# A hybrid diffusion kernel on one core: row broadcasts as two rounded products, adaLN's PSUM bank lent out, heads' transposes in one run, fold's first run and transposes later

## The chip, the cores and the metric

The kernel runs on 1 core of one Trainium2 chip. The metric is the device time of one launch in microseconds (us), the median over runs. All arithmetic is to float32 accuracy. The engines have the profile's names: PE is TensorE (matmuls, with its weight loads as PEld), DVE is VectorE, ACT is ScalarE, POOL is GpSimd, SP is SyncE (which issues most of the transfers).

## The reference, cut to what matters

Two layers over 256 latent tokens and 256 context tokens of width 1024. The first has a convolution mixer, the second a bidirectional mLSTM with four heads of width 512. Each is followed by an MLP of inner width 4096, and each sub-layer is modulated by shifts, scales and gates that adaLN derives from a condition vector. Only the latent tokens are returned.

```python
def adaln(cvec, w, b):
    return jnp.split(jax.nn.silu(cvec) @ w + b, 6, axis=-1)       # sh1, sc1, g1, sh2, sc2, g2

def mlstm_features(u, ...):
    up = u @ w_up
    xm, z = up[..., :MLSTM_INNER], up[..., MLSTM_INNER:]
    xc = jax.nn.silu(dwconv(xm, w_conv) + b_conv)
    q, k, v = xc @ w_q, xc @ w_k, xm @ w_v
    gates = jnp.concatenate([q, k, v], axis=-1) @ w_gate + b_gate
    o = jax.nn.sigmoid(xm @ w_o + b_o)                             # the output gate

def mlstm_output(feats, h_f, h_b, gn_g, skip, w_down):
    hsum = of[..., :MLSTM_INNER] * from_heads(h_f) + of[..., MLSTM_INNER:] * from_heads(h_b)
    hn = normalise(hsum, per head) * gn_g
    return ((hn + skip * xc) * jax.nn.silu(z)) @ w_down

# each layer
h = layer_norm(ALPHA * h + g1 * y, ln1_g[i], ln1_b[i])
h = layer_norm(ALPHA * h + g2 * (jnp.square(jax.nn.relu(modulate(h, sh2, sc2) @ w1)) @ w2), ln2_g[i], ln2_b[i])
```

## The kernel before

**Products.** TensorE multiplies float32 operands either in full precision (tiles of type F32) or rounded (F32R). To keep accuracy in the rounded form, `split` makes of a float32 tile `x` a high part (a cast to F32R on ScalarE, L154) and a low part (`x` less the high part, on VectorE, L155). `mm3t` (L223 to L225) and its sisters (L185, L188, L189; L201, L212) then add up high × high, low × high and high × low in PSUM. Weights come from DRAM into a `raw` tile and are split into `wh` and `wl`, 1024 columns at a time, in four buffers each. A few small products are in full precision: the sums of adaLN, the row broadcasts below, the fold (below), and transposes, which are products with `ident`.

**Order.** Each engine runs its instructions in the order of the built program. The framework's scheduler builds that order from the order in which the code is written, from the buffers (an instruction that writes a tile waits for the last reader of the buffer), and from `tc.issue_after(a)`, which keeps an instruction behind `a`. DMAs on SP are issued in order as well. Generators (`yield`) weave stages into each other step by step: the table `Z.att` names which parts of the output gate (`o0` to `o3`, one for a head), of the scan (`G`, `W`, `A`), and of the down projection (`D0` to `D3`) run together.

**PSUM.** `psum(tag)` hands out banks of 128 × 512 floats: three `mm`, two `ln`, two `cv`, and one, `fl`, which the sums of adaLN and the fold use. A group of products into a bank waits until the last reader of that bank's former content is done.

**Stages,** by the profile's time: adaLN of layer 0 and the convolution's first projection to 150 us, its second projection and the first MLP to 570, the up projections to 690, the v projection (`wv`) to 900, queries, keys and scores head by head to 1182, the output gate together with attention and the down projection to 1453, norm and adaLN's last units to 1459, the last MLP to the end. The change touches these:

- *Fold.* The gates' pre-activations need `w_q` times its part of `w_gate`. Instead of a product with the activations, the kernel multiplies `w_q` transposed (`wqT`) by that part (`wgq`), 16 columns wide and so in four column groups at a time. The `wv` stage has 32 steps of 24 matmuls. `wgq_load` issues one group's loads at steps 1, 5, 12 and 19; `wgq_group(0)` (L876) runs the first group at step 3, and the later ones run further on. `wgq_last`, at step 27, copies the sum out of `fl` on ScalarE (L884) and transposes the copy by four products on PE (L887).
- *Row broadcasts.* `AdaV` gathers adaLN's gate of the second mixer on VectorE in tiles `acc` (S in the profile). `row` (L479) multiplies a full matrix of ones with each, in full precision, which sums over partitions and spreads the sum over all of them; VectorE adds that to the gate's row. It is issued where the output gate begins. `gate2` (L2013) does the same for the last MLP's gate, from the tile `F` and with a column of `fold` as weights, in the second quarter of the last MLP (c = 1).
- *Output gate.* `gate_o(h)` makes for each of two halves (d) a pair of groups (t = 0, 1) of 48 matmuls into two `mm` banks. VectorE reads each bank once, adding a bias (L1752), and ScalarE applies the sigmoid. The three `mm` banks thus serve pairs in turn.
- *Heads.* `attend(h)` normalises the head's output in two blocks (t = 0, 1), scaled on ScalarE (L1806), and transposes them by eight products (L1814) into two `ln` banks, t = 0 first. `down(h)` multiplies the result by `wdown`.
- *Last MLP.* Four quarters (c). `gemm(w1_1, ...)` (L201, L212) produces four blocks each into `mm` banks, which VectorE empties with an addition in `joined` (L218); then `w2_mm` adds into four banks of `ln` and `cv`. The helper `gemm` takes a table `spare` that names another bank for a block.

Of the kernel before, what the change touches and what calls it, by code (L numbers as in the profile page):

```python
# [14 lines left out]
P = 128  # L15
# [56 lines left out]
def hybrid_kernel(ctx: ExitStack, tc: tile.TileContext, xT, vecs_d, taps_d, bdw_d, ada0_w, ada_w, wg_d, pw1a, pw1, pw2, w1_0, w2_0,  # L72
# [61 lines left out]
    nc.gpsimd.iota(fe[:, 0:HL + 1], [[1, HL + 1]], base=0, **exact)  # L134
    ident = con.tile([P, P], F32, name="ident")
    make_identity(nc, ident)
    ones = con.tile([P, P], F32, name="ones")
    nc.vector.memset(ones, 1.0)
    inv_h = con.tile([P, P], F32, name="inv_h")
    nc.vector.memset(inv_h, 1.0 / DH)  # L140
# [80 lines left out]
    def mm3t(ps, xh, xl, wh, wl, start, stop):  # L221

        nc.tensor.matmul(ps, xh, wh, start=start, stop=False)  # L223
        nc.tensor.matmul(ps, xl, wh, start=False, stop=False)  # L224
        nc.tensor.matmul(ps, xh, wl, start=False, stop=stop)  # L225

    def kcol(w, kt):
        if isinstance(w[0], list):
# [183 lines left out]
    class AdaV:  # L412
# [62 lines left out]

        def row(self, i, dst):

            ps = psum()
            nc.tensor.matmul(ps, ones, self.acc[i], start=True, stop=True)  # L479
            nc.vector.tensor_tensor(dst, ps, dst, op=ALU.add)  # L480

    def ad(l, s, which):
        i = ["sh1", "sc1", "g1", "sh2", "sc2", "g2"].index(which)
# [395 lines left out]

    wqs_ps = []  # L880

    def wgq_last():
        qsb = tmp("F")
        nc.scalar.copy(qsb, wqs_ps[0])  # L884
        qtr = psum("fl")
        for b in range(4):
            nc.tensor.transpose(qtr[:, b * P:(b + 1) * P], qsb[:, b * P:(b + 1) * P], ident)  # L887
        nc.vector.tensor_copy(wgp[1].rearrange("p (j b) c -> p j b c", j=4)[:, :, :, 0:16],
                              qtr.rearrange("p (b j c) -> p j b c", b=4, j=4)[:, :, :, 0:16])
# [556 lines left out]
    vstep = 0  # L1446
    for _ in gemm_steps(wv, range(8), xm, T, v_epi):
        vstep += 1
        if vstep in (1, 5, 12, 19):
            wgq_load()  # L1450
        if vstep == 3:
            wgq_group(0)
        if vstep == 27:
            wgq_last()
        if vstep > ET:
            ada_n2.step()
        if vstep in (20, 28):
            xc_load(0 if vstep == 20 else 4)
# [95 lines left out]
    def decay(_):  # L1554
        gT = tmp("L")
        nc.scalar.copy(gT, gps)
        yield
        gk = psum("ln")
        for b in range(4):
            nc.tensor.matmul(gk[:, b * 16:(b + 1) * 16], gT[:, b * P:(b + 1) * P], foldg, start=True, stop=True)  # L1560
        gs = tmp("S")[:, 0:64].rearrange("p (b c) -> p b c", b=4)
        nc.vector.tensor_tensor(gs, gk[:, 0:64].rearrange("p (b c) -> p b c", b=4),
                                VA("b_gate").rearrange("p (b c) -> p b c", b=4), op=ALU.add)
        gb_ = [tmp("L"), tmp("E"), tmp("E")]
        g8 = [gb_[i // 3][:, (i % 3) * 4 * NG:(i % 3 + 1) * 4 * NG].rearrange("p (b c) -> p b c", b=4) for i in range(8)]
        ig, fg, bsb, ex, up1, cor, lf, fa = g8
        nc.vector.memset(ig, 0.0)
        nc.vector.memset(fg, 0.0)
        for d in range(2):
            nc.vector.tensor_copy(ig[:, :, 32 * d:32 * d + 4], gs[:, :, 8 * d:8 * d + 4])  # L1570
            nc.vector.tensor_copy(fg[:, :, 32 * d:32 * d + 4], gs[:, :, 8 * d + 4:8 * d + 8])


        nc.vector.scalar_tensor_tensor(fa, fg, -1.0, fg, op0=ALU.mult, op1=ALU.max)
        nc.scalar.activation(ex, fa, AF.Exp, scale=-1.0)
        nc.vector.tensor_scalar(up1, ex, 1.0, None, op0=ALU.add)
        nc.vector.scalar_tensor_tensor(cor, up1, -1.0, ex, op0=ALU.add, op1=ALU.subtract)
        nc.scalar.activation(lf, up1, AF.Ln)
        nc.vector.reciprocal(up1, up1)
        nc.vector.tensor_tensor(cor, cor, up1, op=ALU.mult)  # L1580
        nc.vector.tensor_tensor(lf, cor, lf, op=ALU.subtract)
        nc.vector.tensor_scalar(fa, fg, 0.0, None, op0=ALU.min)
        nc.vector.tensor_tensor(lf, lf, fa, op=ALU.add)

        nc.vector.memset(up1, 0.0)
        for d, (b0, b1, b2, b3) in ((0, (0, 1, 2, 3)), (1, (1, 0, 3, 2))):
            c = slice(32 * d, 32 if d == 0 else NG)
            nc.vector.tensor_copy(up1[:, b1, c], lf[:, b0, c])
            nc.vector.tensor_tensor(up1[:, b2, c], up1[:, b1, c], lf[:, b1, c], op=ALU.add)
            nc.vector.tensor_tensor(up1[:, b3, c], up1[:, b2, c], lf[:, b2, c], op=ALU.add)  # L1590
        yield
        yield
        yield
        yield
        bps = psum("ln")
        for d, cum in ((0, upper), (1, lower)):
            c = slice(32 * d, 32 if d == 0 else NG)
            reg = bps[:, 0:4 * NG].rearrange("p (b c) -> p b c", b=4)[:, :, c]
            nc.tensor.matmul(reg, cum, lf[:, :, c], start=True, stop=False)
            nc.tensor.matmul(reg, ones, up1[:, :, c], start=False, stop=True)  # L1600
        nc.vector.tensor_copy(bsb, bps[:, 0:4 * NG].rearrange("p (b c) -> p b c", b=4))
        nc.vector.tensor_tensor(acol, ig, bsb, op=ALU.subtract)

        yield
        aT = psum("ln")
        for b in range(4):
            nc.tensor.transpose(aT[:NG, b * P:(b + 1) * P], acol[:, b, :], ident)
        aR, mR = tmp("S"), tmp("S")
        nc.vector.tensor_copy(aR[:32, :], aT[:32, :])
        nc.vector.tensor_copy(aR[32:NG, LO], aT[32:NG, LO])  # L1610
        nc.vector.tensor_copy(aR[32:NG, HI], aT[32:NG, T - 1:C - 1:-1])
        nc.vector.tensor_tensor_scan(mR[:NG, :], aR[:NG, :], aR[:NG, :], 0.0, op0=ALU.max, op1=ALU.max)
        nc.vector.tensor_scalar(negm[:32, :], mR[:32, HI], -1.0, None, op0=ALU.mult)
        nc.vector.tensor_scalar(negm[32:NG, :], mR[32:NG, T - 1:C - 1:-1], -1.0, None, op0=ALU.mult)
        nc.scalar.dma_start(ng_dr, negm)
        bsbs.append(bsb)
        yield
# [112 lines left out]
    def gate_o(h):  # L1730

        for d in range(2):
            bo = rows(BO().rearrange("p a b -> p (a b)"), bo_d[h:h + 1, d * DH:(d + 1) * DH])
            pss = [psum() for _ in range(2)]
            if (h, d) == (1, 1):
                with tc.issue_after(loaded[0]):
                    nc.sync.dma_start(R, r_dr)
            for q in range(4):
                ws = preo if (h, d, q) == (0, 0, 0) else None
                if ws is None:  # L1740
                    raw = raw_load(wo[h, d, q])
                for i in range(2):
                    w = ws[i] if ws else split_w(raw[:, i * 1024:(i + 1) * 1024])
                    for t in range(2):
                        for k in range(2):
                            kt = 4 * q + 2 * i + k
                            sl = slice(k * 512, (k + 1) * 512)
                            mm3t(pss[t], xls[kt][0][:, BLK[t]], xls[kt][1][:, BLK[t]], w[0][:, sl], w[1][:, sl],
                                 kt == 0, kt == ET - 1)
                        if q == 3 and i == 1:  # L1750
                            og[h, d, t] = o_ = OG()
                            nc.vector.tensor_tensor(o_, pss[t], bo, op=ALU.add)  # L1752
                            nc.scalar.activation(o_, o_, AF.Sigmoid)
                    yield
# [12 lines left out]
    def attend(h):  # L1767
# [37 lines left out]
        for t in range(2):  # L1805
            nc.scalar.activation(hs[t], hs[t], AF.Identity, scale=mv[:, t, 2:3], bias=mv[:, t, 3:4])  # L1806
        yield
        yy[h] = []
        for jp in range(2):
            tr = psum("ln")  # L1810
            for jj in range(2):
                j = 2 * jp + jj
                for t in range(2):
                    nc.tensor.transpose(tr[:, jj * C + t * P:jj * C + (t + 1) * P], hs[t][:, j * P:(j + 1) * P], ident)  # L1814
            y = og[h, 1, jp]
            for jj in range(2):
                j, sl = 2 * jp + jj, slice(jj * C, (jj + 1) * C)
# [10 lines left out]
    def down(h):  # L1828
# [13 lines left out]

        def mms(ps, ws, hf, t, first, last):
            for kt in range(4):
                mm3t(ps, yy[h][kt][0][:, BLK[t]], yy[h][kt][1][:, BLK[t]], *ws[hf][kt], first and kt == 0, last and kt == 3)

        if h == 0:
            for hf, ws in enumerate(load()):
# [86 lines left out]
            pre1[m] = split_w(rx[:, (m % 2) * 1024:(m % 2 + 1) * 1024])  # L1935
    ca, cb = comb(1, "ln1_g1", "ln1_b1", "sc2", "sh2", (1,))
    ada_n3 = Ada(1, 10, 2)
    u2 = [X(F32R) for _ in range(DT)]

    def turn(t, g_, tag="ln"):  # L1940
# [69 lines left out]
    def gate2():  # L2010
        for v in range(2):
            ps = psum()
            nc.tensor.matmul(ps, fold[:, 2 * v + 1:2 * v + 2].broadcast_to([P, P]), ada_n3.sb, start=True, stop=True)  # L2013
            nc.vector.tensor_tensor(G2[:, HF[v]], ps, G2[:, HF[v]], op=ALU.add)


# [34 lines left out]
    for c in range(4):  # L2051
# [6 lines left out]
            hid[m] = t_[:, :C], t_[:, C:]  # L2058
            split(*hid[m], q_)

        gemm(w1_1, range(4 * c, 4 * c + 4), u2, T, e1, ko=0 if c else 3 + Z.pre4, pre=pre1 if c == 0 else None)
        if c == 0:
            acc = [[psum("ln") for _ in range(2)], [psum("cv") for _ in range(2)]]
            for i, t_ in enumerate(G5):
                rows(t_, rows_d[i + 1:i + 2])
        elif c < 3:
            if c == 1:
                gate2()
# [142 lines left out]
```

## Time and profile before

| | us |
|---|---|
| median of 3 runs | 1647.28 (1646.98 to 1647.35) |
| profiled execution | 1648.3 |
| its span | 1646.6 |
| PE busy | 1635.1 (99%) |
| DVE busy | 1065.5 (65%) |
| ACT busy | 726.5 (44%) |
| POOL busy | 15.2 (1%) |

The span runs from the first instruction to the last of the profiled execution; 1.7 us of the launch lie outside it. In rows of the timeline the columns are start in us, duration in us, engine, line, operation, output and operands, and how many were run together; in square brackets the idle time before it and what ended it. A full-precision matmul appears as two records. In rows of groups, durations are in ns (least/median/greatest), then first and last start in us. In the list of waits, the numbers are the total in us, how many there were, and the longest.

### The profile page before, as it was taken

The page shows a single profiled execution, that of the slowest core. Times are in us where ns is not written, and L with a number is a line of the kernel's source. Part 1 is how long each engine was busy: PE and PEld are TensorE (multiplying, and loading weights), DVE is VectorE, ACT ScalarE, POOL GpSimd, SP SyncE. Part 2 cuts the span into 40 slices and gives each one's busy share as a digit, 9 for nine tenths or more (in the row PEclk, how much of TensorE's full clock was granted, in tenths as well). Part 3 has the DMA queues.
Part 4 walks back from the last instruction along what each step waited for, and adds up shares of the span by engine and source line. Part 5 has one row for each costly group of instructions (what it writes and reads, how often), then busy time and mean ns, then how long its engine had stood idle before and what let it go on. Part 6 is the DMA issues. An engine that isn't in the chain of part 4 may idle for free. (4 is left out here: it accounts for less than half of the span.)

```text
span 1646.6 us, 22777 instructions
## 1 busy us (share of the span) xinstructions
PE 1635.1 (99%) x8794; PEld 1354.3 (82%) x8794; DVE 1065.5 (65%) x1916; ACT 726.5 (44%) x1170; POOL 15.2 (1%) x67
## 2 busy tenths in 40 slices
PE   9999999999999999999999999999999999999998
PEld 6675998888888998877787899888878888878887
DVE  7697886666535876762444753653489776776677
ACT  4313762322324485642223532433478654555453
POOL 0000000000000000000000000000000000000001
PEclk9999999999999999999999999999999999999999
DMA  9766223434323166596684842553466565675452
GB/s 353 259 217 243 91 101 121 140 132 148 127 90 141 38 222 197 175 308 220 232 270 141 299 157 103 179 199 122 172 206 227 208 216 207 235 291 182 180 189 92
DMA packets 87548, 305.82 MB, mean 186 GB/s; under 512 B 12780, under 2 KB 31120, under 8 KB 59536
## 3 DMA queue, kind: packets, MB, share of 16 engines
q1 hardware_dynamic: 64976, 288.07, 49.9%
q10 hardware_dynamic: 22464, 16.30, 3.2%
q8 instruction: 69, 1.13, 0.3%
q14 instruction: 39, 0.32, 0.1%
HBM read 286.47 MB, written 17.86 MB: 185 GB/s over the span
## 5 line engine op out<-in xcount | busy, mean ns | idle before, releaser
L155 DVE TENSOR_TENSOR wl<-raw,wh 128x1024 fp32r<-128x1024 f32 x344 | 418.6, 1221 | 254.8 <-ACT wh L154 250.6
L154 ACT CAST wh<-raw 128x1024 fp32r<-128x1024 f32 x344 | 358.9, 1051 | 497.9 <-PE mm L188 311.9
L188 PE MATMUL mm<-u,wh 128*128 128x512 f32 (+1 forms) x802 | 288.8, 361 | 0.0
L185 PE MATMUL mm<-u,wh 128*128 128x512 f32 (+1 forms) x674 | 239.8, 356 | 0.0
L189 PE MATMUL mm<-u,wl 128*128 128x512 f32 (+1 forms) x674 | 238.5, 355 | 0.0
L188 PEld LDWEIGHTS mm<-u,wh 128*128 128x128 f32 x802 | 151.2, 189 | 23.1 <-issue 0.8
L185 PEld LDWEIGHTS mm<-u,wh 128*128 128x128 f32 x674 | 127.3, 189 | 21.5 <-issue 2.4
L189 PEld LDWEIGHTS mm<-u,wl 128*128 128x128 f32 x674 | 127.2, 189 | 18.4 <-issue 0.8
L223 PE MATMUL mm<-wh,xl 128*128 128x512 f32 x256 | 101.1, 395 | 0.6 <-DVE og L1752 0.6
L185 PE MATMUL mm<-xm,wh 128*128 128x512 f32 x256 | 100.1, 391 | 0.0
L224 PE MATMUL mm<-wh,xl 128*128 128x512 f32 x256 | 100.0, 391 | 0.0
L189 PE MATMUL mm<-xm,wl 128*128 128x512 f32 x256 | 99.6, 389 | 0.0
L225 PE MATMUL mm<-wl,xl 128*128 128x512 f32 x256 | 99.3, 392 | 0.1
L185 PE MATMUL mm<-hid,wh 128*128 128x512 f32 (+1 forms) x256 | 93.3, 365 | 0.0
L189 PE MATMUL mm<-hid,wl 128*128 128x512 f32 (+1 forms) x256 | 92.8, 363 | 0.0
L188 PE MATMUL mm<-hid,wh 128*128 128x512 f32 (+1 forms) x256 | 92.8, 363 | 0.0
L188 PE MATMUL mm<-qq,wh 128*128 128x272 f32 x256 | 73.9, 289 | 0.0
L185 PE MATMUL mm<-qq,wh 128*128 128x272 f32 x256 | 73.5, 288 | 0.0
L189 PE MATMUL mm<-qq,wl 128*128 128x272 f32 x256 | 73.5, 288 | 0.0
L1258 DVE SCALAR_TENSOR_TENSOR x<-mm,ada,x 128x256 f32<-128x256 f32 x64 | 28.5, 479 | 62.9 <-PE mm L189 62.8
L1381 DVE SCALAR_TENSOR_TENSOR E<-pad,vecs,E 128x512 f32<-128x512 f32 x64 | 47.9, 749 | 27.9 <-ACT E L1379 26.7
L185 PEld LDWEIGHTS mm<-xm,wh 128*128 128x128 f32 x256 | 48.0, 188 | 13.3 <-issue 3.4
(572 smaller groups left out, 3185.9 us busy)
## 6 DMA issues: line engine op xcount, KB each, us to landing
raw<-w SPq DMA_DIRECT2D x64, 1024.0 KB, 4.8
raw<-wo SPq DMA_DIRECT2D x32, 1024.0 KB, 4.8
raw<-ada_w SPq DMA_DIRECT2D x22, 1024.0 KB, 6.1
ar<-ada_w SPq DMA_DIRECT2D x80, 256.0 KB, 3.6
raw<-wv SPq DMA_DIRECT2D x16, 1024.0 KB, 7.4
raw<-wq SPq DMA_DIRECT2D x16, 1024.0 KB, 5.1
raw<-wk SPq DMA_DIRECT2D x16, 1024.0 KB, 5.4
u<-wqT SPq DMA_DIRECT2D x56, 256.0 KB, 6.0
```

The source lines that it names most:

```text
L154: c = nc.scalar.copy(hi, src)
L155: lastsub[0] = nc.vector.tensor_tensor(lo, src, hi.bitcast(F32), op=ALU.subtract).ins
L185: a = nc.tensor.matmul(ps, wh, xh, start=start, stop=False)
L188: nc.tensor.matmul(ps, wh, xl, start=False, stop=False)
L189: lastmm[0] = nc.tensor.matmul(ps, wl, xh, start=False, stop=stop).ins
L223: nc.tensor.matmul(ps, xh, wh, start=start, stop=False)
L224: nc.tensor.matmul(ps, xl, wh, start=False, stop=False)
L225: nc.tensor.matmul(ps, xh, wl, start=False, stop=stop)
L1258: nc.vector.scalar_tensor_tensor(res[m][:, sl_], p_, g[:, m:m + 1], res[m][:, sl_], op0=ALU.mult, op1=ALU.add)
L1381: nc.vector.scalar_tensor_tensor(s2_(acc), pad[:, :, k:k + C], V("w_conv", m * QTAP + k), s2_(acc), op0=ALU.mult, op1=ALU.add)
```

## The change

- The broadcast by `row` and by `gate2` becomes two rounded products: the rows are split into a high and a low part, and both are multiplied by a rounded matrix of ones (`ones_r`, `fold_r`), whose values are exact in that type. `gate2`'s split is made in the quarter before.
- `gate_o` puts its second group (t = 1) of the second half (d = 1) into `fl`, except for head 2; the last MLP puts block 4 of its numbering of the first quarter there.
- In `attend` the transposes take t = 1 first and are tied so that all eight of a bank pair follow the first; head 3's wait for a mark in head 2's down projection.
- The fold's first run moves from step 3 to 4 of the `wv` stage, its second group's loads from 5 to 6; the copy stays at step 27, now written by itself, and its transposes move to 30.
- The gates' matmuls in `decay` are tied behind the output gate's first product.

```diff
--- before.py
+++ after.py
@@ -134,7 +134,8 @@
     nc.gpsimd.iota(fe[:, 0:HL + 1], [[1, HL + 1]], base=0, **exact)
     ident = con.tile([P, P], F32, name="ident")
     make_identity(nc, ident)
-    ones = con.tile([P, P], F32, name="ones")
+    ones_r = con.tile([P, P], F32R, name="ones")
+    ones = ones_r.bitcast(F32)
     nc.vector.memset(ones, 1.0)
     inv_h = con.tile([P, P], F32, name="inv_h")
     nc.vector.memset(inv_h, 1.0 / DH)
@@ -222,7 +223,7 @@
 
         nc.tensor.matmul(ps, xh, wh, start=start, stop=False)
         nc.tensor.matmul(ps, xl, wh, start=False, stop=False)
-        nc.tensor.matmul(ps, xh, wl, start=False, stop=stop)
+        return nc.tensor.matmul(ps, xh, wl, start=False, stop=stop).ins
 
     def kcol(w, kt):
         if isinstance(w[0], list):
@@ -475,9 +476,14 @@
 
         def row(self, i, dst):
 
-            ps = psum()
-            nc.tensor.matmul(ps, ones, self.acc[i], start=True, stop=True)
-            nc.vector.tensor_tensor(dst, ps, dst, op=ALU.add)
+            spread(ones_r, self.acc[i], (tmp("E", F32R), tmp("E", F32R)), dst)
+
+    def spread(w, rows_, parts, dst):
+        split(*parts, rows_)
+        ps = psum()
+        for k, part_ in enumerate(parts):
+            nc.tensor.matmul(ps, w, part_, start=k == 0, stop=k == 1)
+        nc.vector.tensor_tensor(dst, ps, dst, op=ALU.add)
 
     def ad(l, s, which):
         i = ["sh1", "sc1", "g1", "sh2", "sc2", "g2"].index(which)
@@ -879,9 +885,12 @@
 
     wqs_ps = []
 
+    def wgq_copy():
+        wqs_ps.append(tmp("F"))
+        nc.scalar.copy(wqs_ps[1], wqs_ps[0])
+
     def wgq_last():
-        qsb = tmp("F")
-        nc.scalar.copy(qsb, wqs_ps[0])
+        qsb = wqs_ps[1]
         qtr = psum("fl")
         for b in range(4):
             nc.tensor.transpose(qtr[:, b * P:(b + 1) * P], qsb[:, b * P:(b + 1) * P], ident)
@@ -1446,11 +1455,13 @@
     vstep = 0
     for _ in gemm_steps(wv, range(8), xm, T, v_epi):
         vstep += 1
-        if vstep in (1, 5, 12, 19):
+        if vstep in (1, 6, 12, 19):
             wgq_load()
-        if vstep == 3:
+        if vstep == 4:
             wgq_group(0)
         if vstep == 27:
+            wgq_copy()
+        if vstep == 30:
             wgq_last()
         if vstep > ET:
             ada_n2.step()
@@ -1557,7 +1568,8 @@
         yield
         gk = psum("ln")
         for b in range(4):
-            nc.tensor.matmul(gk[:, b * 16:(b + 1) * 16], gT[:, b * P:(b + 1) * P], foldg, start=True, stop=True)
+            with tc.issue_after(mark["o"]):
+                nc.tensor.matmul(gk[:, b * 16:(b + 1) * 16], gT[:, b * P:(b + 1) * P], foldg, start=True, stop=True)
         gs = tmp("S")[:, 0:64].rearrange("p (b c) -> p b c", b=4)
         nc.vector.tensor_tensor(gs, gk[:, 0:64].rearrange("p (b c) -> p b c", b=4),
                                 VA("b_gate").rearrange("p (b c) -> p b c", b=4), op=ALU.add)
@@ -1731,7 +1743,7 @@
 
         for d in range(2):
             bo = rows(BO().rearrange("p a b -> p (a b)"), bo_d[h:h + 1, d * DH:(d + 1) * DH])
-            pss = [psum() for _ in range(2)]
+            pss = [psum(), psum("fl" if d and h != 2 else "mm")]
             if (h, d) == (1, 1):
                 with tc.issue_after(loaded[0]):
                     nc.sync.dma_start(R, r_dr)
@@ -1745,8 +1757,9 @@
                         for k in range(2):
                             kt = 4 * q + 2 * i + k
                             sl = slice(k * 512, (k + 1) * 512)
-                            mm3t(pss[t], xls[kt][0][:, BLK[t]], xls[kt][1][:, BLK[t]], w[0][:, sl], w[1][:, sl],
-                                 kt == 0, kt == ET - 1)
+                            a = mm3t(pss[t], xls[kt][0][:, BLK[t]], xls[kt][1][:, BLK[t]], w[0][:, sl], w[1][:, sl],
+                                     kt == 0, kt == ET - 1)
+                            mark.setdefault("o", a)
                         if q == 3 and i == 1:
                             og[h, d, t] = o_ = OG()
                             nc.vector.tensor_tensor(o_, pss[t], bo, op=ALU.add)
@@ -1805,13 +1818,20 @@
         for t in range(2):
             nc.scalar.activation(hs[t], hs[t], AF.Identity, scale=mv[:, t, 2:3], bias=mv[:, t, 3:4])
         yield
+        while h == H - 1 and "down" not in mark:
+            yield
         yy[h] = []
+        lead = mark["down"] if h == H - 1 else None
         for jp in range(2):
             tr = psum("ln")
             for jj in range(2):
                 j = 2 * jp + jj
-                for t in range(2):
-                    nc.tensor.transpose(tr[:, jj * C + t * P:jj * C + (t + 1) * P], hs[t][:, j * P:(j + 1) * P], ident)
+                for t in (1, 0):
+                    with tc.issue_after(lead) if lead else nullcontext():
+                        a = nc.tensor.transpose(tr[:, jj * C + t * P:jj * C + (t + 1) * P], hs[t][:, j * P:(j + 1) * P],
+                                                ident)
+                    if jj == 0 and t == 1:
+                        lead = a.ins
             y = og[h, 1, jp]
             for jj in range(2):
                 j, sl = 2 * jp + jj, slice(jj * C, (jj + 1) * C)
@@ -1842,7 +1862,10 @@
 
         def mms(ps, ws, hf, t, first, last):
             for kt in range(4):
-                mm3t(ps, yy[h][kt][0][:, BLK[t]], yy[h][kt][1][:, BLK[t]], *ws[hf][kt], first and kt == 0, last and kt == 3)
+                a = mm3t(ps, yy[h][kt][0][:, BLK[t]], yy[h][kt][1][:, BLK[t]], *ws[hf][kt], first and kt == 0,
+                         last and kt == 3)
+            if (h, hf, t) == (2, 0, 0):
+                mark["down"] = a
 
         if h == 0:
             for hf, ws in enumerate(load()):
@@ -1935,6 +1958,8 @@
             pre1[m] = split_w(rx[:, (m % 2) * 1024:(m % 2 + 1) * 1024])
     ca, cb = comb(1, "ln1_g1", "ln1_b1", "sc2", "sh2", (1,))
     ada_n3 = Ada(1, 10, 2)
+    fold_r = con.tile([P, 16], F32R, name="fold_r")
+    nc.vector.tensor_copy(fold_r, fold)
     u2 = [X(F32R) for _ in range(DT)]
 
     def turn(t, g_, tag="ln"):
@@ -2010,7 +2035,8 @@
     def gate2():
         for v in range(2):
             ps = psum()
-            nc.tensor.matmul(ps, fold[:, 2 * v + 1:2 * v + 2].broadcast_to([P, P]), ada_n3.sb, start=True, stop=True)
+            for k in range(2):
+                nc.tensor.matmul(ps, fold_r[:, 2 * v + 1:2 * v + 2].broadcast_to([P, P]), parts[k], start=k == 0, stop=k == 1)
             nc.vector.tensor_tensor(G2[:, HF[v]], ps, G2[:, HF[v]], op=ALU.add)
 
 
@@ -2058,11 +2084,14 @@
             hid[m] = t_[:, :C], t_[:, C:]
             split(*hid[m], q_)
 
-        gemm(w1_1, range(4 * c, 4 * c + 4), u2, T, e1, ko=0 if c else 3 + Z.pre4, pre=pre1 if c == 0 else None)
+        gemm(w1_1, range(4 * c, 4 * c + 4), u2, T, e1, ko=0 if c else 3 + Z.pre4, pre=pre1 if c == 0 else None,
+             spare={} if c else {4: "fl"})
         if c == 0:
             acc = [[psum("ln") for _ in range(2)], [psum("cv") for _ in range(2)]]
             for i, t_ in enumerate(G5):
                 rows(t_, rows_d[i + 1:i + 2])
+            parts = tmp("S", F32R), tmp("L", F32R)
+            split(*parts, ada_n3.sb)
         elif c < 3:
             if c == 1:
                 gate2()
```

Where the new order differs on PE, at three places. The names are those of the output and the two operands with their numbers, then the shape. First the fold's first run in the `wv` stage: the last matmuls ahead of it, before,

```order
3629 L185 MATMUL mm_6697<-xm_6675,wh_6791 128x512
3630 L188 MATMUL mm_6697<-x_6676,wh_6791 128x512
3631 L189 MATMUL mm_6697<-xm_6675,wl_6792 128x512
3632 L876 MATMUL fl_6821<-u_6729,wgq_593 32x512
3633 L876 MATMUL fl_6821<-u_6730,wgq_593 32x512
```

and after:

```order
3653 L186 MATMUL mm_6698<-xm_6675,wh_6821 128x512
3654 L189 MATMUL mm_6698<-x_6676,wh_6821 128x512
3655 L190 MATMUL mm_6698<-xm_6675,wl_6822 128x512
3656 L882 MATMUL fl_6851<-u_6729,wgq_593 32x512
3657 L882 MATMUL fl_6851<-u_6730,wgq_593 32x512
```

It stands 24 matmuls further on; the weights of the matmul ahead of it are the next step's (`wh_6821` for `wh_6791`).

Second the output gate, where the pair of head 1's first half begins (the bracket names the engine on which an instruction waits), before,

```order
6354 L225 MATMUL mm_11034<-wl_11227,xl_10784 128x512
6355 L223 MATMUL mm_11250<-wh_11254,xl_10737 128x512 [waits Activation_49]
6356 L224 MATMUL mm_11250<-wh_11254,xl_10737 128x512
6357 L225 MATMUL mm_11250<-wl_11255,xl_10737 128x512 [waits DVE_49]
6358 L223 MATMUL mm_11250<-wh_11254,xl_10740 128x512
6359 L224 MATMUL mm_11250<-wh_11254,xl_10740 128x512
6360 L225 MATMUL mm_11250<-wl_11255,xl_10740 128x512
6361 L223 MATMUL mm_11250<-wh_11280,xl_10743 128x512 [waits Activation_49]
6362 L224 MATMUL mm_11250<-wh_11280,xl_10743 128x512
6363 L223 MATMUL mm_11251<-wh_11254,xl_10737 128x512 [waits DVE_49]
```

and after:

```order
6356 L226 MATMUL fl_11044<-wl_11237,xl_10794 128x512
6357 L224 MATMUL mm_11260<-wh_11264,xl_10747 128x512 [waits Activation_49]
6358 L225 MATMUL mm_11260<-wh_11264,xl_10747 128x512
6359 L226 MATMUL mm_11260<-wl_11265,xl_10747 128x512 [waits DVE_49]
6360 L224 MATMUL mm_11260<-wh_11264,xl_10750 128x512
6361 L225 MATMUL mm_11260<-wh_11264,xl_10750 128x512
6362 L226 MATMUL mm_11260<-wl_11265,xl_10750 128x512
6363 L224 MATMUL mm_11261<-wh_11264,xl_10747 128x512
```

The group of block t = 1 (`mm_11251`, now `mm_11261`) no longer waits for DVE, and starts six matmuls behind the first in place of eight.

Third the transposes of head 0, before,

```order
6412 L225 MATMUL mm_11250<-wl_11482,xl_10781 128x512
6413 L1814 MATMUL ln_11457<-ident,og_11005 128x128
6414 L1814 MATMUL ln_11469<-ident,og_11005 128x128
6415 L223 MATMUL mm_11250<-wh_11481,xl_10784 128x512
6416 L224 MATMUL mm_11250<-wh_11481,xl_10784 128x512
6417 L1814 MATMUL ln_11457<-ident,og_11014 128x128
6418 L1814 MATMUL ln_11457<-ident,og_11005 128x128
6419 L1814 MATMUL ln_11457<-ident,og_11014 128x128
6420 L1814 MATMUL ln_11469<-ident,og_11014 128x128
6421 L1814 MATMUL ln_11469<-ident,og_11005 128x128
6422 L1814 MATMUL ln_11469<-ident,og_11014 128x128
```

and after:

```order
6416 L225 MATMUL mm_11260<-wh_11491,xl_10794 128x512
6417 L226 MATMUL mm_11260<-wl_11492,xl_10794 128x512
6418 L1831 MATMUL ln_11467<-ident,og_11024 128x128
6419 L1831 MATMUL ln_11467<-ident,og_11015 128x128
6420 L1831 MATMUL ln_11467<-ident,og_11024 128x128
6421 L1831 MATMUL ln_11467<-ident,og_11015 128x128
6422 L1831 MATMUL ln_11479<-ident,og_11024 128x128
6423 L1831 MATMUL ln_11479<-ident,og_11015 128x128
6424 L1831 MATMUL ln_11479<-ident,og_11024 128x128
6425 L1831 MATMUL ln_11479<-ident,og_11015 128x128
6426 L224 MATMUL mm_11261<-wh_11491,xl_10791 128x512
```

One transpose of each bank stood two matmuls ahead of the other six; now all eight stand in a row.

## The prediction

> **What bounds the kernel now.** I read the head of the page first: is one engine busy throughout, and at what clock?
>
> ```profile
> span 1646.6 us, 22777 instructions
> ...
> PE 1635.1 (99%) x8794; PEld 1354.3 (82%) x8794; DVE 1065.5 (65%) x1916; ACT 726.5 (44%) x1170; POOL 15.2 (1%) x67
> ...
> PEclk9999999999999999999999999999999999999999
> ...
> PE 20%; DVE 0%; DMA 0%; ACT 0%; issue 0%; DVEq 0%; ACTq 0%
> ```
>
> TensorE (PE) is busy for 99% of the span, at full granted clock in all 40 slices, and no other engine has a percent of the chain that ended last. So a change gains only where it shortens PE's own work or one of its few waits, and loses where it makes PE wait. Next I took the list of PE's waits by releaser:
>
> ```profile
> PE ln L1814 <- ACT og L1806: 0.6, 1, 0.6
> PE mm L223 <- DVE og L1752: 0.6, 2, 0.3
> PE fl L887 <- ACT F L884: 0.6, 1, 0.6
> ...
> PE mm L201 <- DVE E L218: 0.3, 1, 0.3
> ```
>
> These four are places that the change touches, and together they are only 2.1 us. A matmul that stands with its weights loaded counts as busy, however. So I read the timeline place by place. Undisturbed 512-column rounded matmuls start 0.227 us apart (1209.17, 1209.40, 1209.62 in Part 4), and whatever is more than that I count as loss.
>
> **Part 1: fold's first run, 24 matmuls later.** The rows of line L876, in a window on its first run and in one on its second:
>
> ```profile
> L876 PE MATMUL fl<-u,wgq x32: 592/592/617, 721.8 to 726.5; 128*32 128x512 f32 x32
> ...
> DMA u<-wqT: 2.1, 4
> ```
>
> ```profile
> L876 PE MATMUL fl<-u,wgq x32: 592/592/592, 771.7 to 774.7; 128*32 128x512 f32 x32
> ```
>
> It is the same 32 records both times, but their starts spread over 4.7 us in the first run and over 3.0 in the second. The first run stands four times for transfers of `u<-wqT`. When its last matmul started, at 726.5, all of them had landed. Moved by 24 matmuls (24 × 0.227 = 5.45 us) it starts at 721.8 + 5.45 = 727.2, after that, and should go like the second run. That is −1.7 us. The ends are 0, if the transfers come later too, and −2.1, the whole wait. They were issued into buffers that were free before the run, so I see no reason for the first, and take −1.7. The next group of loads is issued one step (5.45 us) later, when this run has freed its buffers. It is used at 771.7, some 40 us on: hidden.
>
> **Part 2: fold's transposes, with the copy ahead.** Rows of PE, then ScalarE's:
>
> ```profile
> 872.43 0.40 PE L185 MATMUL mm<-xm,wh 128*128 128x512 f32 x1
> 873.38 0.66 PE L887 MATMUL fl<-ident,F 128*128 128x128 f32 x4 [0.55 <-ACT F L884]
> ```
>
> ```profile
> 872.74 0.58 ACT L884 COPY F<-fl 128x512 f32<-128x512 f32 x1
> ```
>
> The transposes could have started at 872.43 + 0.23 = 872.66 and started at 873.38, when the copy had ended at 873.32: 0.72 lost. The copy stays at step 27 of the stage and the transposes go to step 30, so three steps of 24 matmuls, 16 us, lie between. I take −0.7, with ends 0 and −0.8 (a restart of some 0.1 with it, sized in Part 4).
>
> **Part 3: the row broadcasts, in two places.** The first stands where the output gate begins. PE's rows there and 7 us on, then VectorE's:
>
> ```profile
> 1181.86 1.88 PE L479 MATMUL mm<-S,ones 128*128 128x512 f32 x4
> ...
> 1183.81 0.40 PE L224 MATMUL mm<-wh,xl 128*128 128x512 f32 x1
> ...
> 1191.04 0.50 PE L225 MATMUL mm<-wl,xl 128*128 128x512 f32 x1
> ```
>
> ```profile
> 1182.98 1.52 DVE L155 TENSOR_TENSOR xl<-raw,xl 128x256 fp32r<-128x256 f32 x4 [6.39 <-ACT xl L154]
> ...
> 1189.78 1.21 DVE L155 TENSOR_TENSOR wl<-raw,wh 128x1024 fp32r<-128x1024 f32 x1
> ```
>
> Two full-precision products are four records. With one rounded matmul of the gate behind them they end at 1183.81, so they take 1183.81 − 0.23 − 1181.86 = 1.72 us, 0.43 a record. Four rounded products take 4 × 0.227 = 0.91. That is −0.81 of PE's work. The Trainium skill, "FP8 and Floating Point Precision" (TensorE Precision Notes), says that a true FP32 product takes four passes through the array. At the trace's 0.227 a pass that is an estimate of 0.91 per product, where the trace shows 0.86, and the gain would be 0.91 instead of 0.81.
>
> But here the gain has nowhere to go. VectorE began the `xl` splits at 1182.98 on a cast that ScalarE makes once it is through with the scores, and the change moves neither. And at 1191.04 PE read the low half of a weight that VectorE finished at 1189.78 + 1.21 = 1190.99. PE comes 0.81 earlier and waits 0.81 longer. The ends are −0.81 and 0, and I take 0, since PE stands on VectorE at that point already.
>
> The broadcast's own splits are two casts on ScalarE and two subtractions on VectorE, in the scores stage. VectorE idles there for 6.39 us at the end of it (row at 1182.98), so they cost 0, unless they block a queue (rival d).
>
> The second broadcast is in the last MLP, shown with VectorE's weight splits just ahead:
>
> ```profile
> 1526.81 1.88 PE L2013 MATMUL mm<-F,fold 128*128 128x512 f32 x4
> ...
> 1528.76 0.40 PE L224 MATMUL ln<-wh,hid 128*128 128x512 f32 x1
> ```
>
> ```profile
> 1522.83 1.22 DVE L155 TENSOR_TENSOR wl<-raw,wh 128x1024 fp32r<-128x1024 f32 x1
> 1525.62 1.23 DVE L155 TENSOR_TENSOR wl<-raw,wh 128x1024 fp32r<-128x1024 f32 x1
> ```
>
> Again 1528.76 − 0.23 − 1526.81 = 1.72 against 0.91. Here VectorE makes a weight every 2.79 us with 1.23 us of work, so it can follow, and the gain stays: −0.81, with ends −0.81 and 0. The splits of this place and the rounded copy of `fold` are three operations of the kind that take 0.4 to 0.8 us, where VectorE has more than half of its time free: 0.
>
> **Part 4: the gate's second bank.** PE's rows at three groups' starts, with VectorE's row that belongs to 1237.06:
>
> ```profile
> 1209.17 0.39 PE L223 MATMUL mm<-wh,xl 128*128 128x512 f32 x1
> 1209.40 0.39 PE L224 MATMUL mm<-wh,xl 128*128 128x512 f32 x1
> 1209.62 0.39 PE L225 MATMUL mm<-wl,xl 128*128 128x512 f32 x1
> 1210.06 0.50 PE L223 MATMUL mm<-wh,xl 128*128 128x512 f32 x1
> ...
> 1232.67 0.39 PE L224 MATMUL mm<-wh,xl 128*128 128x512 f32 x1
> 1233.28 0.50 PE L223 MATMUL mm<-wh,xl 128*128 128x512 f32 x1 [0.22 <-DVE og L1752]
> 1233.61 0.40 PE L224 MATMUL mm<-wh,xl 128*128 128x512 f32 x1
> ...
> 1237.06 0.39 PE L225 MATMUL cv<-wl,pw 128*128 128x512 f32 x1
> ...
> 1288.87 0.39 PE L225 MATMUL mm<-wl,xl 128*128 128x512 f32 x1
> 1289.60 0.50 PE L223 MATMUL mm<-wh,xl 128*128 128x512 f32 x1 [0.34 <-DVE og L1752]
> ```
>
> ```profile
> 1235.34 1.21 DVE L155 TENSOR_TENSOR wl<-raw,wh 128x1024 fp32r<-128x1024 f32 x1
> ```
>
> Steps of 0.44, 0.61 and 0.73 us stand where 0.23 would, which is 0.21 + 0.38 + 0.50. The restart costs 0.1 more each time (1233.28 to 1233.61 is 0.33): 0.3 + 0.5 + 0.6 = 1.4 us. In the new order none of the three matmuls waits for VectorE's addition. What is late next is the weights: 1235.34 + 1.21 = 1236.55 for a matmul at 1237.06, a slack of 0.51. So of the 0.8 from the first two waits I keep 0.5, and the third whole: −1.1. The ends are 0 and −1.4.
>
> **Part 5: the heads' transposes.** The fourth head, PE and then ScalarE:
>
> ```profile
> 1432.97 0.44 PE L1814 MATMUL ln<-ident,og 128*128 128x128 f32 x2 [0.57 <-ACT og L1806]
> ```
>
> ```profile
> 1432.11 1.52 ACT L1806 ACTIVATE og<-og,gmv 128x512 f32<-128x512 f32 x2 [0.43 <-DVE gmv L1803]
> ```
>
> PE waits until 1432.97 for the first half of ScalarE's scaling, does two transposes and two matmuls, and then the other six. The new order fills 0.68 us of that wait with three matmuls, but begins with the second block, whose half ends at 1432.11 + 1.52 = 1433.63. The six started after the second half now as well, so the wait is filled by three matmuls instead of two matmuls and two transposes: 0, with ends −0.6 (the wait's row) and +0.3. In the other heads only the place of a few rows changes: 0.
>
> There is a rule that speaks against gathering transposes: the Trainium skill, "TensorE: Matmul & The Clock Gate" (Part 4: PE-mode transpose), has it that they do not count as PE work for the clock gate. The granted clock above shows no dip at the runs of six, so no term changes.
>
> **Part 6: the last MLP's spare bank.**
>
> ```profile
> 1470.72 0.40 PE L212 MATMUL cv<-x,wh 128*128 128x512 f32 x1
> 1471.43 0.70 PE L201 MATMUL mm<-x,wx 128*128 128x512 f32 x2 [0.32 <-DVE E L218]
> ```
>
> 0.71 stands where 0.23 would, and with a restart of 0.1 that is −0.6. adaLN's bank has no reader open by then in the new order. Ends 0 and −0.6.
>
> Sum: −1.7 − 0.7 − 0.8 − 1.1 − 0.6 = −4.9 us. The profiled execution took 1648.3 us (the span and 1.7 around it), 1.0 above the median of 1647.28. Against the median that is 1642.4.
>
> **Rivals.**
> (a) The attention stage keeps nothing, because VectorE is its bound and takes back all of Part 4: −4.9 + 1.1 = −3.8, 1643.5. For it speaks the slack of 0.51; against it the third wait, 50 us further on, at which PE is itself the late one.
> (b) VectorE's work moves up with PE's, and Part 3's first place and all of Part 4 are kept: −4.9 − 0.8 − 0.3 = −6.0, 1641.3. Against it stands the wait at 1191.04.
> (c) The first run still waits for its transfers, which share a queue with the weights, and its transposes lose as much elsewhere: −4.9 + 1.7 + 0.7 = −2.5, 1644.8.
> (d) Slower: the new casts of the broadcast's rows stand in ScalarE's queue in the scores stage, and what they read comes late there:
>
> ```profile
> DVE S L439 <- DMA ar<-ada_w: 21.5, 14, 3.1
> ```
>
> VectorE's sums, which the casts read, wait up to 3.1 us for one transfer. A cast at the head of ScalarE's queue then holds back the casts of `rr` behind it, and the scores' matmuls behind those. This decides the sign once PE has to stand for over 4.9 us. Two whole waits, 6.2 us, would give 1642.4 + 6.2 = 1648.6. Against it: there are two casts, and the waits list has no wait of PE in that stage, so PE has something in hand.
> (e) No effect: each gain is lost at the next late operand, 1647.3. Against it stand the stages of Parts 1, 2 and 6, where no wait but the one removed is listed.
>
> **How the numbers follow.** Likeliest 0.47 (its own range 1641.7 to 1643.2), (a) 0.17, (b) 0.12, (c) 0.12, (d) 0.06, (e) 0.06. A measurement of this kernel can tell 0.2%, 3.3 us, from no change, so faster means below 1644.0: 0.47 + 0.17 + 0.12 = 0.76. Same is (c) and (e), 0.18. Slower is (d), 0.06. The range leaves out (d), (e) and the far part of (b): 1640.6 to 1645.4.
>
> **What would show it.** Right: the waits on `og` L1752 at these three places, `F` L884 and `E` L218 are gone, and the one on the heads' transposes stays. Fold's first run spreads over 3.0 us. The broadcasts step 0.227, and PE waits some 0.8 us longer at the weight of 1191.04. Wrong: the first run still stands for `u<-wqT`, PE waits in the scores stage, or the gates' weights end later than they do now.

## The result, and the profile after

The changed kernel took 1643.8 us (1643.38 to 1646.23, 19 runs) against 1646.79 (1645.23 to 1648.56, 19 runs) of the kernel before: a ratio of 0.9983, 95% interval 0.9977 to 0.9989, or −2.8 us (−3.8 to −1.8). The forecast was −4.9, or 1642.4. The direction was right, and about 60% of the amount came: the time lies inside the forecast's range (1640.6 to 1645.4), but outside that of its likeliest case (1641.7 to 1643.2).

The head of the page after, then the full list of PE's waits:

```profile
span 1642.7 us, 22786 instructions
...
PE 1631.3 (99%) x8794; PEld 1354.1 (82%) x8794; DVE 1068.1 (65%) x1920; ACT 729.4 (44%) x1173; POOL 15.2 (1%) x67
...
PEclk9999999999999999999999999999999999999999
```

```profile
PE fl L224 <- DVE E L1876: 1.2, 1, 1.2
PE cv L180 <- DVE ones L139: 1.1, 1, 1.1
PE ln L1831 <- ACT og L1819: 0.3, 1, 0.3
PE ln L225 <- DVE hid L156: 0.3, 1, 0.3
PE mm L226 <- DVE wl L156: 0.2, 1, 0.2
```

Three of the four waits shown before are gone (the gate's addition, the copy `F`, `joined`'s `E`), and the heads' (L1831 now) is 0.3 instead of 0.6 in this execution. The head of the list is new: 1.2 us, once, for the addition that empties `fl` in head 0's down projection (L1876). The last two of the list are dealt with below. The wait for `WCS` (a tile of the first stage), 0.5 us before, is off the list as well; it lies in the first 9 us, where the change touches nothing but the type of `ones`.

Where the time went is best seen by comparing the start of each matmul in both traces and looking for the places where the difference steps. The forecast's places in the trace of after, fold's first run as a group of its line, then rows of PE's timeline:

```profile
L882 PE MATMUL fl<-u,wgq x32: 592/592/617, 726.7 to 729.8; 128*32 128x512 f32 x32
```

```profile
885.86 0.60 PE L896 MATMUL fl<-ident,F 128*128 128x128 f32 x4
...
1178.86 1.09 PE L485 MATMUL mm<-E,ones 128*128 128x512 f32 x4
...
1188.05 0.50 PE L226 MATMUL mm<-wl,xl 128*128 128x512 f32 x1 [0.24 <-DVE wl L156]
...
1206.56 0.39 PE L226 MATMUL mm<-wl,xl 128*128 128x512 f32 x1
1206.79 0.39 PE L224 MATMUL fl<-wh,xl 128*128 128x512 f32 x1
...
1430.53 1.09 PE L1831 MATMUL ln<-ident,og 128*128 128x128 f32 x8 [0.34 <-ACT og L1819]
...
1523.09 0.39 PE L2039 MATMUL mm<-S,fold_r 128*128 128x512 f32 x1
...
1524.02 0.39 PE L224 MATMUL ln<-wh,hid 128*128 128x512 f32 x1
```

Fold's first run spreads over 3.1 us instead of 4.7, the transposes of its copy have no idle time before them, a gate's second group starts 0.23 after the matmul ahead of it, and the second broadcast takes 1524.02 − 1523.09 = 0.93 instead of 1.72. All that came as forecast. PE is ahead of the trace of before by 3.0 us when the queries are done, by 4.5 at 1316, and then, at 1332 of before, by only 3.1. Of the 3.0, 0.5 is there from the first 9 us on and can't be put down to the change: the first product with `WCS` starts at 9.25 before and at 8.67 after, but in the traces of these experiments anywhere from 8.47 to 9.25 with the old type of `ones` and from 8.66 to 9.24 with the new. Nothing in the forecast stands at that place.

**The new wait.** PE, VectorE, ScalarE and SP there, in the trace after:

```profile
1326.82 0.39 PE L226 MATMUL fl<-wl,og 128*128 128x512 f32 x1
...
1329.36 0.50 PE L224 MATMUL fl<-wh,og 128*128 128x512 f32 x1 [1.25 <-DVE E L1876]
```

```profile
1317.44 1.28 DVE L1765 TENSOR_TENSOR og<-mm,bo 128x512 f32<-128x512 f32 x2
...
1327.47 1.23 DVE L156 TENSOR_TENSOR wl<-raw,wh 128x1024 fp32r<-128x1024 f32 x1 [2.21 <-ACT wh L155]
1328.62 0.68 DVE L1876 TENSOR_TENSOR E<-fl,G 128x512 f32<-128x512 f32 x1
```

```profile
1326.39 1.05 ACT L155 CAST wh<-raw 128x1024 fp32r<-128x1024 f32 x1 [2.75 <-DMA raw<-wdown]
```

```profile
1315.82 0.33 SPq L149 DMA_DIRECT2D raw<-wdown  x1
1318.75 0.33 SPq L1667 DMA_DIRECT2D bo<-bo_d  x1
1319.17 0.38 SPq L149 DMA_DIRECT2D raw<-wdown  x1
```

And SP, ScalarE and VectorE before:

```profile
1319.45 2.10 SPq L148 DMA_DIRECT2D raw<-wdown  x2
1322.99 0.33 SPq L1655 DMA_DIRECT2D bo<-bo_d  x1
```

```profile
1328.75 1.05 ACT L154 CAST wh<-raw 128x1024 fp32r<-128x1024 f32 x1 [1.40 <-PE mm L224]
```

```profile
1331.66 0.69 DVE L1853 TENSOR_TENSOR E<-fl,G 128x512 f32<-128x512 f32 x1 [0.59 <-PE fl L225]
```

Before, both halves of head 0's down weights were issued together, and the bias row of the gate's pair (2, 1) behind them; ScalarE's cast waited for PE and not for the transfer, and VectorE's addition waited for PE. Now the bias row stands between the halves. Its one buffer comes free with VectorE's two additions (1317.44 + 1.28 = 1318.72), so SP stands until 1318.75 and issues the second half at 1319.17, 3.4 us behind the first instead of 1.8. ScalarE waits 2.75 us for it. VectorE has the low half of that weight in its queue ahead of the addition that empties `fl`, and stands 2.21 us. PE needs the bank, and stands 1.25.

### The profile page after: what moved, and what is told of

It is laid out like the page before. It is cut to its first block, busy times and chain, and to the rows that moved or that the text cites. A ratio compares the mean times of both kernels' runs of the same rounds, so it can differ in the third digit from the quotient of the medians.

```text
span 1642.7 us, 22786 instructions
## 1 busy us (share of the span) xinstructions
PE 1631.3 (99%) x8794; PEld 1354.1 (82%) x8794; DVE 1068.1 (65%) x1920; ACT 729.4 (44%) x1173; POOL 15.2 (1%) x67
## 5 line engine op out<-in xcount | busy, mean ns | idle before, releaser
L224 PE MATMUL mm<-wh,xl 128*128 128x512 f32 x208 | 81.7, 394 | 0.1
L225 PE MATMUL mm<-wh,xl 128*128 128x512 f32 x208 | 81.4, 391 | 0.0
L226 PE MATMUL mm<-wl,xl 128*128 128x512 f32 x208 | 80.6, 391 | 0.2 <-DVE wl L156 0.2
L186 PEld LDWEIGHTS mm<-xm,wh 128*128 128x128 f32 x256 | 48.0, 188 | 13.2 <-issue 2.5
```

Of the source, the lines that this page charges most:

```text
L186: a = nc.tensor.matmul(ps, wh, xh, start=start, stop=False)
L226: return nc.tensor.matmul(ps, xh, wl, start=False, stop=stop).ins
```

## The experiments

Theory A: the swap on SP's queue cost the missing time, and the transposes part brought it with it. Rival B: the down projection would have absorbed the gain anyway, since its weights do not move up with PE. All times are ratios to the kernel before on the same chip.

**The bias row behind both halves again,** all else as in the changed kernel:

```diff
+            late = 2 if (h, d) == (2, 1) else 0
+            if not late:
                 bo = rows(BO()..., bo_d[...])
...
             for q in range(4):
+                if late and q == late:
+                    with tc.issue_after(loaded[0]):
+                        bo = rows(BO()..., bo_d[...])
```

> The changed kernel, with the bias row of the gate's last pair but two (h, d) = (2, 1) loaded after the second half of head 0's down weights again, as in the kernel before; nothing else differs in any queue. Theory A (the swap on SP's queue makes the 1.2 us wait at head 0's down projection): that wait goes, PE gains 1.2 to 1.4 us on the changed kernel, so -4.2 to -4.4 us against the kernel before instead of -3.0. Rival B (the down projection absorbs it: PE comes 1.5 us earlier than before onto weights and a VectorE that do not move up): the wait stays within 0.3 us, -3.0 to -3.3.

1642.13 us (1641.61 to 1642.9), ratio 0.9971 (0.9961 to 0.9981). SP, ScalarE and VectorE at that place:

```profile
1315.93 1.50 SPq L149 DMA_DIRECT2D raw<-wdown  x2
1318.86 0.33 SPq L1667 DMA_DIRECT2D bo<-bo_d  x1
```

```profile
1324.71 1.05 ACT L155 CAST wh<-raw 128x1024 fp32r<-128x1024 f32 x1 [0.94 <-DMA raw<-wdown]
```

```profile
1327.35 0.69 DVE L1881 TENSOR_TENSOR E<-fl,G 128x512 f32<-128x512 f32 x1 [0.32 <-PE fl L226]
```

The cast is 1.7 us earlier than in the trace after, and the addition now waits for PE instead of PE for it. The wait of 1.2 is off the list. A holds, B does not.

**The changed kernel again,** as yardstick.

> The changed kernel itself, as the yardstick on the same chip: -3.0 us against the kernel before under either theory. Its trace also shows what belongs to one execution only: at the last MLP's end PE lost 0.6 us at 1617.70 in the first trace, where the last weights' transfer landed 6.9 us after its issue instead of 6.0. If this is the transfer's own spread, it is not there again; if it is the change's new order on VectorE, it is.

1643.57 us (1643.14 to 1644.48), ratio 0.9982 (0.9974 to 0.9991). The kernel above is 1.4 us faster on the same chip, and the two ranges do not touch. The 1.2 us wait is there again, the 0.3 for `hid` at the end is not, and the last weights' transfer landed 6.06 us after its issue instead of 6.91. So the 0.6 lost at the end belonged to the first execution.

**The swap alone,** in the kernel before:

```diff
-            bo = rows(BO()..., bo_d[...])
+            bo = BO()...
+            mark["bo"] = nc.sync.dma_start(bo, bo_d[...].broadcast_to([P, DH])).ins
...
-                raw = raw_load(wdown[h, hf])
+                with tc.issue_after(mark["bo"]) if (h, hf) == (0, 1) else nullcontext():
+                    raw = raw_load(wdown[h, hf])
```

> The kernel before with only the swap on SP's queue: the second half of head 0's down weights is issued after the bias row of (2, 1); no other queue differs. Theory A: issued some 2 us later, its high half comes that much later, and VectorE, which has its low half ahead of the addition that empties fl, comes late to it: +0.6 to +1.4 us, with a wait of PE for the line of that addition (L1853). Rival B: within 0.3 us of the kernel before, no such wait.

1648.26 us (1647.68 to 1649.45), ratio 1.0010 (1.0001 to 1.0019): +1.6 us. Its list of PE's waits begins with

```profile
PE fl L223 <- DVE E L1855: 1.2, 1, 1.2
```

One load issued in another place makes the whole wait, without any of the change's gains. Together with the first experiment, in which the wait went and the gain stayed, that excludes B.

**The transposes part undone,** and **the transposes part alone:**

> The changed kernel without the heads' transposes part (attend and the mark in down as before); the loads on SP then stand as before too at that place. Theory A: the transposes part brought the swap with it, so without it -4.0 to -4.4 us against the kernel before (it gives up the 0.3 us that the fourth head's transposes gained). Rival B: -2.7 to -3.1.

1642.58 us (1641.73 to 1643.6), ratio 0.9976 (0.9966 to 0.9986): −4.0 us, as A had it, though the interval alone (−5.6 to −2.3) leaves room for B. SP issues both halves ahead of the bias row again (1314.51 and 1316.28, then 1318.05), and the wait of 1.2 is off the list of PE's waits.

> The kernel before with only the heads' transposes part. It brings the swap on SP's queue with it. Theory: +1.5 from the swap (as measured alone) and -0.3 from the fourth head's transposes, +0.9 to +1.4 us. Rival, the prediction's Part 5 without the swap: -0.6 to +0.3.

1648.33 us (1647.36 to 1649.55), ratio 1.0009 (1.0000 to 1.0018), with the bias row (1321.23) between the halves (1318.29 and 1321.65) and the same wait at the head of its list:

```profile
PE fl L223 <- DVE E L1863: 1.2, 1, 1.2
```

So it is this part that moves the load. Nothing of it is written for SP; the scheduler put the bias row earlier when the transposes were tied otherwise. Why it did so was not tried. Whether the transposes themselves gain anything stays open: with the swap mended they are worth 1642.13 against 1642.58, and those two ranges overlap. The wait of the fourth head's transposes settles nothing either: it varies from execution to execution, in the old order between none and 0.7 us, in the new one between 0.2 and 0.6 (0.3 and 0.5 in the two traces of the changed kernel).

**The other parts alone,** each in the kernel before.

> The kernel before with only fold's first run, loads and transposes moved (and a copy of its own). The prediction's Parts 1 and 2: -1.7 - 0.7 = -2.4 us; a little less, -2.0, if 0.4 us of the first run's wait belonged to the profiled execution alone (in the trace of the kernel before with the swap alone, the same run is 0.4 us shorter). Rival: the weights behind the moved run's loads come late in turn, and less than -1.2 is left.

1644.72 us, ratio 0.9987 (0.9978 to 0.9995): −2.1 us. The rival, under 1.2, is at odds with it but not excluded by the interval; the trace shows no new wait in the `wv` stage.

> The kernel before with only the gate's second groups in adaLN's bank and the gates' matmuls tied behind the output gate's first. The prediction's Part 4: -1.1 us, of which 0.6 from the third wait, at 1289. Rival: that wait belonged to the profiled execution alone (in the trace of the kernel before with the swap alone, PE is 0.6 us earlier from there on, with no change at that place), and -0.3 to -0.6 is left.

1646.13 us, ratio 0.9994 (0.9985 to 1.0003): −1.0 us, which this measurement can't tell from 0 or from −2. The trace settles the rest. The row that made the third wait is ScalarE's cast of a weight, in the trace of before and in that of the kernel with the last MLP's edits alone (next), which is the same up to there:

```profile
1285.16 1.05 ACT L154 CAST wh<-raw 128x1024 fp32r<-128x1024 f32 x1 [2.88 <-DMA raw<-v_dr]
```

```profile
1282.12 1.05 ACT L154 CAST wh<-raw 128x1024 fp32r<-128x1024 f32 x1 [1.15 <-DMA raw<-v_dr]
```

The transfer landed 7.1 us after its issue in the first and 4.8 in the second. In the second, PE runs past 1289 without a step over 0.23, and so it does in the traces of the swap alone and of the transposes alone. So the third wait, 0.6 us of the forecast, was a late transfer in one execution and not the kernel's habit.

> The kernel before with only the last MLP's two edits: its fourth block in adaLN's bank, and the second row broadcast as two rounded products. The prediction's Parts 3 (second place) and 6: -0.6 - 0.8 = -1.4 us. Rival: the last MLP's end is set by the transfers of its weights, which do not move up as far, and -0.7 or less is left.

1645.99 us, ratio 0.9993 (0.9984 to 1.0002): −1.2 us, unclear by its interval. In its trace PE gains 0.58 at the spare bank and 0.81 at the broadcast, and gives 0.2 back at the end.

> The kernel before with only the first row broadcast (start of the output gate) as two rounded products. The prediction's Part 3: 0, since VectorE sets the pace there; within 0.3 us of the kernel before. Rival (its case b): PE keeps what it saves, -0.8 us.

1646.2 us, ratio 0.9996 (0.9987 to 1.0005): no change that can be told. Since 0.8 us is inside such an interval too, the place itself was tested with PE's work there taken away. This kernel leaves out the sum over partitions (VectorE adds the unsummed rows to the gate's row), so its output is not the reference's:

```diff
-            ps = psum()
-            nc.tensor.matmul(ps, ones, self.acc[i], start=True, stop=True)
-            nc.vector.tensor_tensor(dst, ps, dst, op=ALU.add)
+            nc.vector.tensor_tensor(dst, self.acc[i], dst, op=ALU.add)
```

> The kernel before without the first row broadcast's products: VectorE adds the rows to the gate's row unsummed, so the mLSTM's output gate of adaLN is not the reference's. It tells what the place can give at all: PE has 1.72 us less to do there. If VectorE sets the pace, 0 to -0.3 us; if PE does, -1.7.

1646.24 us, ratio 0.9998 (0.9989 to 1.0007), and at the head of PE's waits

```profile
PE mm L225 <- DVE wl L155: 1.3, 1, 1.3
```

PE has 1.72 us less to do at 1182 and stands 1.3 longer 7 us later, for the same weight that the forecast named. The interval would still allow a gain, but the traces show none: PE leads the trace of before by 1.3 us when it comes to this place and by 1.3 us when that weight is through, and with the two rounded products alone by 1.05 and 1.07.

## Why the prediction was right, and where it was off

- **Part 1 (−1.7) and Part 2 (−0.7): right in mechanism, Part 1 too large.** The start of the run came at 726.7 (727.2 was forecast), the spread fell to 3.1, and in the trace PE gains 1.7 there and 0.8 at the transposes. Both alone measure −2.1 (−3.6 to −0.8). But the first spread, 4.7 or rather 4.8 (from 721.76 to 726.54), was the longest seen: in six other traces with the old order there (swap, gate's bank, last MLP, transposes and row alone, row removed) it is 4.0 to 4.4. So 0.4 to 0.8 us of the wait belonged to one execution, and 1.0 to 1.3 to the kernel.
- **Part 3: right in what both places gain.** The first gains 0.24 at once and nothing by 1190, the second 0.81. The weight of which Part 3 said that PE would wait there does stop it, but only 0.2 us longer than before and not 0.8: the rest was lost ahead of it, where the first gate matmuls start 0.45 and 0.35 us apart instead of 0.23. At the second place Part 3 took VectorE to be more than half free; it was busy for 13.2 of the 15 us from 1515 to 1530, and the gain stayed all the same. By the Trainium skill's four passes ("FP8 and Floating Point Precision", TensorE Precision Notes) the estimate for the second would have been 0.91; the trace shows 0.81.
- **Part 4 (−1.1): right in mechanism, too large.** All three waits are gone, but the third was worth 0.6 in the profiled execution alone. In the trace of the gate's bank alone PE gains 0.27 at the first and 0.51 at the second and gives 0.14 back right after: 0.6 of the 0.8, near the 0.5 that the slack of the weight allowed.
- **Part 5 (0): this is the step that failed.** On PE's own rows nothing speaks against it: the wait ahead of the fourth head's transposes stays, and no gain or loss there stands out of its spread. But the step said that "in the other heads only the place of a few rows changes: 0", and read only PE's and ScalarE's rows. The part also moves a transfer on SP past another, which no term of the sum had. It measured +1.6 alone, and its removal gave 1.4: most of the 2.1 that are missing. The other part are waits of one execution, 0.6 of Part 4 and 0.4 to 0.8 of Part 1. As an estimate from the traces, the kernel's own gains are 1.0 to 1.3, 0.7, 0.8, 0.6 and 0.6 (Parts 1, 2, 3, 4, 6), which is 3.7 to 4.0; less 1.4 to 1.6 for the swap this leaves 2.1 to 2.6, inside the measured interval.
- **Part 6 (−0.6): right,** 0.57 in the trace of after and 0.58 in that of the last MLP's edits alone.
- **The baseline.** The profiled execution of before stands 1.5 us above the later median, of which 0.6 is the late `v_dr` transfer, 0.4 or more the wait in fold's first run, and 0.5, against the trace of after, the late start in the first 9 us. The forecast named the distance and took the waits out of it all the same.
- **The rivals.** The result lies closest to (a), 1643.5, but not by its mechanism: the attention stage kept the gains of Part 4 and lost 1.4 us at another place. What (a) said of the third wait, that PE is itself the late one there, was wrong: VectorE was late, behind the cast that waited for `v_dr`. Rival (b) needed the first broadcast to pay, (c) the first run to wait, (d) ScalarE to block; no run shows one of them.
- **The Trainium skill's rule on transposes** ("TensorE: Matmul & The Clock Gate", Part 4: PE-mode transpose): eight in a row take 0.84 us (1430.53 to 1431.37), and the granted clock of the page after shows no dip in any of its 40 slices. It had no bearing, as forecast.

The fastest version of these runs is the changed kernel with the bias row behind both halves: −4.8 us by its ratio, with an interval of −6.4 to −3.1. That this meets the forecast's −4.9 so closely is in part luck, since 1 us or more of the forecast's terms were waits of one execution.

## What to carry to other kernels

Where a scheduler sets the order, compare every queue before and after, the transfers' too, and give each moved transfer a price: what it now stands behind, when that one's buffer comes free, and who waits for what lands. In a kernel whose TensorE is 99% busy small waits are most of the gain, and here one transfer in the wrong place took about a third of it back. A wait of one profiled execution is not yet a wait of the kernel: where its cause is a transfer's landing, look for it in a second execution before it enters the sum.

## What was not expected of the hardware

The same transfer can land at quite different times from one execution to the next. In the changed kernel itself, the last MLP's last weights landed 6.91 us after their issue in one execution and 6.06 in another, and PE lost 0.6 us in the first. The load from `v_dr` took 7.1 us in one execution and 4.8 in another of programs that are the same up to there, and this too moved PE by 0.6 us. (The casts that wait for it, at 1285.16 and 1282.12, are further apart because PE and the issue were already ahead in the second.) With fold's first run and the start, such places may make up most of the 1.5 us by which the first profiled execution stood above the median.
